# Two weight sums of each MLP half moved from VectorE to adding DMAs on GpSimd's queue, and a new order of the down products

## The chip, the cores and the metric

The kernel runs on one core of one Trainium2 chip. The metric is the device time of one execution in microseconds (us); lower is better. The engines are TensorE (PE, its weight loads PEld), VectorE (DVE), ScalarE (ACT), GpSimd (POOL) and SyncE (SP), each with an instruction stream that it works off in order, and 16 DMA engines that move data between the chip's memory and the on-chip buffers.

## The reference, cut to what matters

A trunk of two decoder layers over 512 tokens of width 1024: layer 0 mixes with multi-head latent attention, layer 1 with gated linear attention; behind each mixer stands an MLP with 4096 hidden units.

```
def sq_relu_mlp(xn, w_up, w_down):
    hid = jnp.square(jax.nn.relu(xn @ w_up))
    return hid @ w_down
...
x = x + mix
x = x + sq_relu_mlp(rms_norm(x, norm_mlp[i]), mlp_w_up[i], mlp_w_down[i])
```

The change touches the two MLPs alone (and the helper that prepares their inputs).

## The kernel before, in words

Every float32 operand of a large matmul is split into a high and a low part (`split`, L112 and L115): ACT copies the operand to the rounded type (`wh`), and DVE subtracts that copy from the operand (`wl`). Three matmuls (high by high, high by low, low by high) then stand for one. `piece` does this for one weight tile; it has three buffers for `wh` and `wl`.

The MLP takes its 4096 hidden units in 8 blocks of 512 (numbered b = 0 to 7), and multiplies in the seven-product scheme of Strassen and Winograd, which needs sums of quarters of the weight matrix. A weight block is cut into quarters: "11" (upper rows, first columns), "12" (lower rows, first columns), "21" (upper rows, second columns) and "22" (lower rows, second columns); in the code `a11`, `a12`, `a21`, `a22` for the up weights.

**Up, per block.** `up_block` gives a list of steps, s1, s5, s2, s6, s3, s7, s4, each with one product of 24 matmuls (L818, 128x128 weights by 256 columns). Its weights are, in turn: a11; `s` = a21 + a22 (summed by DVE, L904, in s5); a12; `s` - a11 (L919, s6); a12 - `s` (L925, s3); a11 - a21 (L932, s7); a22 (s4). Each quarter is 512 KB and is loaded by SP (L852) into one of five buffers (`raw`); a load waits until its buffer's last reader is done. For blocks 0 and 1 the quarters a21 and a22 come together, in one 1 MB load (L1116) into a buffer of the down weights, which are free at that time. Behind the products DVE forms the hidden values (L862, L928, L935: rectified and scaled by the token's `rstd`) and ACT squares them (L863). s4's product goes on in the PSUM bank that s7's product left, so it can begin only when DVE has read that bank in L935.

**Down, per two blocks.** `down_block` has seven products of 48 matmuls, p1, p5, p6, p7, p2, p3, p4, on quarters of 1 MB (SP, L950, three buffers). DVE sums weights for four of them: L987 ("21" + "22" into `S`), L992 (`S` - "11"), L1004 ("11" - "21"), L1019 ("12" - `S`), and hidden values for four (L988, L993, L1005, L1024). There are three such blocks per MLP; the last two hidden blocks go through plain matmuls.

The steps of up and down are interleaved by a fixed list: while down block s is multiplied, up blocks 2s+2 and 2s+3 are. The order on each engine is that in which the code issues; `issue_after` and `keep_in_program_order` pin single places. The layers' inputs for the seven products (`T0` to `T3`, four chunks of sums of token halves) are made in `combine` (L294 to L301) during the output projection before the MLP.

Of the kernel before, what the change touches and what calls it, by code (L numbers as in the profile page):

```python
# [49 lines left out]
def trunk_kernel(ctx: ExitStack, tc: tile.TileContext, t_in: dict, out: bass.AP, out_row: bass.AP):  # L50
# [40 lines left out]
    PADS = dict(stage=224, right=64, up=320, masks=256, keep=128, hidden=(0, 0), down_w=(224, 224))  # L91

    def pad(pool, n):
        if n:
# [3 lines left out]
        pad(opened("stage"), PADS["stage"])  # L98

    opened_stage()  # L100
    pad(opened("edge", "right"), PADS["right"])
    opened("wide", "right")
    opened("ps", space=bass.MemoryType.PSUM)

# [102 lines left out]
    def gcol(name, j):  # L207
        c = GAIN_COL[name] + j
        return gains[:, c : c + 1]
# [56 lines left out]
    class QuadNorm(Norm):  # L266
# [24 lines left out]

        def combine(self, k, t):
            g1, g2 = (gcol(self.g, self.g0 + j) for j in (k, k + KH))
            u, v = xT[k], xT[k + KH]  # L294
# [3 lines left out]
            DVE.scalar_tensor_tensor(t2, u[:, first], g1, t3, ALU.mult, ALU.add)  # L298
            DVE.scalar_tensor_tensor(t4, v[:, first], g2, t2, ALU.mult, ALU.subtract)
            DVE.scalar_tensor_tensor(t1, v[:, second], g2, t2, ALU.mult, ALU.subtract)  # L300
            return t  # L301

        def difference(self, k):
            DVE.tensor_tensor(xT[k][:, second], xT[k][:, second], xT[k + KH][:, second], ALU.subtract)

        def combined(self, k, t):
            pool = pool_of("up")
# [478 lines left out]
    def out_proj(w2d, X, nxt, after, begun=None):  # L786
        for c in range(4):
            if c == 0:
                ps_, rest = begun or out_start(w2d, X, 0)
                rest()  # L790
            else:
                w = out_cols(w2d, c)
                if c == 3:
                    next(after)
                ps_ = [bank("ac"[c % 2]), bank("ac"[c % 2])]
                for j in range(2):
                    a_type(ps_[j], w[j], X)
            for j in range(2):
                m = c + j * KH
                DVE.tensor_tensor(xT[m], ps_[j], xT[m], ALU.add)  # L800
                nxt.add(m, xT[m])
            if c < 3:
                nxt.pair(c)
                nxt.difference(c)


    def mlp(layer, nrm, nxt, final=False):
# [2 lines left out]
        NB = FF // FB  # L810
        up = pool_of("up")

        def wide_raw():
            return pool_of("down_w").tile([P, 4, 512], F32, tag="raw", bufs=3, name=uname("raw"))

        def matmuls(p, w, k0, ks, ms, x, begin, end):
            def one(i, j, k, m, start, stop):
# [15 lines left out]
            for k, m in steps:  # L833
                one(1, 0, k, m, False, end and k == 3)

        Q, wide, turn = {}, {}, [0, 1]

        def up_block(b):
            fh, s = b % 2, b // 2
# [6 lines left out]
            def unit(half, trail):  # L846
                if half and b < 2:
                    return wide[b][:, trail * KH : trail * KH + KH]
                t = up.tile([P, KH, 256], F32, tag="raw", bufs=5, name=uname("raw"))
                c0 = b * FB + half * 256  # L850
                with tc.issue_after(wide["last"].ins) if wide else nullcontext():
                    SP.dma_start(t, w_up[trail * 512 : trail * 512 + 512, c0 : c0 + 256].rearrange("(k p) n -> p k n", p=P))  # L852
                return t

            def product(p, a, name, begin):
                w = v.pop(name) if name in v else piece(a, KH, 256)
# [2 lines left out]
            def finish(c, half, tk):  # L859
                qs = q[tk is second][:, 2 * half : 2 * half + 2]  # L860
                r = nrm.rstd[:, tk].unsqueeze(1).to_broadcast([P, 2, TH])
                DVE.scalar_tensor_tensor(qs, c, 0.0, r, ALU.max, ALU.mult)  # L862
                ACT.activation(qs, qs, AF.Square)  # L863

            def pairs(t):
# [33 lines left out]

            def s5():  # L900
                s = v["s"] = up.tile([P, KH, 256], F32, tag="raw", bufs=5, name=uname("raw"))
                if "a12" not in v:
                    v["a12"] = unit(0, 1)
                DVE.tensor_tensor(s, v["a21"], v["a22"], ALU.add)  # L904
# [11 lines left out]
            def s6():  # L916
                if b == 1:
                    seed(v["p1"])
                DVE.tensor_tensor(v["s"], v["s"], v["a11"], ALU.subtract)  # L919
                product(v["b2"], v["s"], "T2", False)  # L920
                v["u2"] = mt()
                ACT.activation(v["u2"], v["b2"], AF.Copy)

            def s3():
                DVE.tensor_tensor(v["a12"], v["a12"], v["s"], ALU.subtract)  # L925
                product(v["x5"], v["a12"], "22", False)
                c = q[1][:, 0:2]
                DVE.tensor_tensor(c, pairs(v["x5"]), pairs(v["u2"]), ALU.add)  # L928
                finish(c, 0, second)

            def s7():
                DVE.tensor_tensor(v["a21"], v["a11"], v["a21"], ALU.subtract)  # L932
                product(v["b2"], v["a21"], "T3", False)
                c = q[1][:, 2:4]
                DVE.tensor_tensor(c, pairs(v["b2"]), pairs(v["p5"]), ALU.add)  # L935
                finish(c, 1, second)
# [7 lines left out]
        def down_block(s):  # L944
            last = s == NB // 2 - 2

            def quarter(dh, fh):
                t = wide_raw()
                r0 = (2 * s + fh) * FB
                SP.dma_start(t, w_dn[r0 : r0 + FB, dh * 512 : dh * 512 + 512].rearrange("(k p) n -> p k n", p=P))  # L950
                return t

            def operand(t):
# [7 lines left out]
            def product(n, a, t, evac=None):  # L961
                x = operand(t)
                p = mp.tile([P, 4 * TH], F32, tag="d", bufs=2, name=uname("ps"))
                p4 = p.rearrange("p (m t) -> p m t", m=4)
                begin = s == 0
                if not begin:
                    ACT.activation(p4, acc[n], AF.Copy)
                for h in range(2):
                    w = piece(a[:, 2 * h : 2 * h + 2], 2, 512)
                    matmuls(p, w, 2 * h, (2 * h, 2 * h + 1), range(4), x, begin, True)  # L970
                if evac is not None:
                    evac(p4)
                elif begin and n in (2, 3, 4, 5):
                    DVE.tensor_tensor(acc[n], p4, acc[n], ALU.add)
                else:
                    ACT.activation(acc[n], p4, AF.Copy)

# [1 line left out]
            (b11, b12), (b21, b22) = Q[s, 0], Q[s, 1]  # L979

            def p1():
                v["11"] = quarter(0, 0)
                product(1, v["11"], b11)

            def p5():
                v["21"], v["S"] = quarter(1, 0), quarter(1, 1)
                DVE.tensor_tensor(v["S"], v["21"], v["S"], ALU.add)  # L987
                DVE.tensor_tensor(b11, b12, b11, ALU.subtract)  # L988
                product(5, v["S"], b11)

            def p6():
                DVE.tensor_tensor(v["S"], v["S"], v["11"], ALU.subtract)  # L992
                DVE.tensor_tensor(b11, b22, b11, ALU.subtract)  # L993

                def u2(p4):
                    DVE.tensor_tensor(acc[6], p4, acc[1], ALU.add)
# [4 lines left out]
                product(6, v["S"], b11, u2 if last else None)  # L1001

            def p7():
                DVE.tensor_tensor(v["21"], v["11"], v["21"], ALU.subtract)  # L1004
                DVE.tensor_tensor(b12, b22, b12, ALU.subtract)  # L1005

                def u3(p4):
# [3 lines left out]

                product(7, v["21"], b12, u3 if last else None)

            def p2():
                v["12"] = quarter(0, 1)
                product(2, v["12"], b21)

            def p3():
                DVE.tensor_tensor(v["S"], v["12"], v["S"], ALU.subtract)  # L1019
                product(3, v["S"], b22)  # L1020

            def p4():
                a = quarter(1, 1)
                DVE.tensor_tensor(b21, b21, b11, ALU.subtract)  # L1024
                product(4, a, b21)

            return [p1, p5, p6, p7, p2, p3, p4]

        def hidden(b, pool):
            n = 1 if final else 2  # L1030
# [11 lines left out]
        def down(b, hid):  # L1042
            for c in range(2):
                raw = raw_rows(b, c)
                for g in range(2):
# [3 lines left out]
                    for j in range(2):  # L1049
                        m = c * 4 + g * 2 + j  # L1050
                        p = bank("b")
                        a_type(p, w, hid, cols=slice(j * P, (j + 1) * P))
                        DVE.tensor_tensor(xT[m], p, xT[m], ALU.add)
                        if b == NB - 1:
                            nxt.add(m, xT[m])

# [54 lines left out]
            x = quad["11"][0][0]  # L1111
            PE.matmul(t[:, h * TH : (h + 1) * TH], x[:, :P], x, start=h == 0, stop=True, skip_group_check=True)
        for b in range(2):
            t = wide[b] = wide_raw().rearrange("p a (b n) -> p (a b) n", b=2)
            c0 = b * FB + 256
            wide["last"] = SP.dma_start(t, w_up[:, c0 : c0 + 256].rearrange("(k p) n -> p k n", p=P))  # L1116
        kept = tc.keep_in_program_order
        for b in range(2):
            blocks[b].pop(0)()
# [4 lines left out]
        kept(nrm.combined(KH - 1, t))  # L1124
        pad(up, PADS["up"])
        nrm.finish()
        nrm.difference(KH - 1)
        for b in range(2):
            blocks[b].pop(0)()
        downs = []  # L1130
# [419 lines left out]
    turns = rope_turns()  # L1550

    O, begun = mla(0, nrm, w0, mla_pools)
    rope_es.close()
# [160 lines left out]
```

## Time and profile before

| what | value |
|---|---|
| time, median of 3 runs | 1083.45 us (1081.42 to 1085.34) |
| the profiled execution's own time | 1080.79 us |
| its span, first to last instruction | 1079.1 us |
| mean granted TensorE clock | 0.997 |
| PE busy | 1058.9 us (98%), 7322 matmuls |
| DVE busy | 890.0 us (82%) |
| ACT busy | 640.2 us (59%) |
| POOL busy | 44.5 us (4%) |
| moved by DMA | 107.88 MB, mean 100 GB/s |

The span is the time on the engines; the device time is 1.7 us longer. The page gives for each engine its busy time and share, then groups of equal instructions; "idle before" is how long an engine stood still just before an instruction, and behind the arrow stands what it waited for. Layer 0's MLP lies at about 193 to 450 us of the span, layer 1's at about 746 to 1006 us.

### The profile page before, as it was taken

The numbers are of one execution on the slowest core, as the hardware profiler recorded it, in microseconds if no ns is written. First come the engines' busy times: TensorE is split into PE (matmuls) and PEld (weight loads), VectorE is DVE, ScalarE is ACT, GpSimd is POOL, SyncE is SP. The second block draws the span as 40 slices with busy tenths as digits, with TensorE's granted clock in tenths as the row PEclk, the third lists the DMA queues.
The fourth block names the chain that finished last, engine by engine and source line by source line (L and its number), as shares of the span: only waits on it lengthen the run. The fifth ranks groups of instructions, "written<-read, shape, count | busy, mean of one in ns | idle before, by whom it ended". The sixth has DMA issues, their size and how long they took to land.

```text
span 1079.1 us, 17824 instructions
## 1 busy us (share of the span) xinstructions
PE 1058.9 (98%) x7322; PEld 977.1 (91%) x7322; DVE 890.0 (82%) x1210; ACT 640.2 (59%) x934; POOL 44.5 (4%) x78
## 2 busy tenths in 40 slices
PE   9999999989999999999999999999899999999997
PEld 7788888989999999988788888888899999999986
DVE  6789879999899899967565655678999899899865
ACT  6577655566667776644334735655565667766734
POOL 6400000000000000030000000000000000000000
PEclk9999999999999999999999999999999999999999
DMA  7312017143433433260222222234324423522412
GB/s 211 95 49 79 13 31 229 42 136 99 157 98 99 157 100 96 86 203 24 62 67 78 79 79 57 61 98 138 117 79 129 146 82 134 176 76 82 137 39 79
DMA packets 97969, 107.88 MB, mean 100 GB/s; under 512 B 8048, under 2 KB 72832, under 8 KB 97888
## 3 DMA queue, kind: packets, MB, share of 16 engines
q1 hardware_dynamic: 95872, 105.52, 31.1%
q8 instruction: 57, 0.93, 0.4%
q10 hardware_dynamic: 1952, 1.21, 0.4%
q0 software_dynamic: 64, 0.02, 0.1%
q14 instruction: 24, 0.20, 0.1%
HBM read 104.64 MB, written 2.10 MB: 99 GB/s over the span
## 4 chain that ended last, share of the span: by engine, by line
PE 84%; DVE 11%; issue 2%; ACT 2%; DMA 1%; SPq 0%; DVEq 0%; ACTq 0%
PE ps L818 39%; PE ps L120 12%; PE ps L122 12%; PE ps L121 12%; DVE wl L115 4%; PE ps L137 2%; PE ps L1371 2%; DMA wraw_ckv<-in_mla_w_in_dram 1%; DVE q L862 1%; DVE h L115 1%; DVE raw L925 1%; ACT wh L112 1%; DVE raw L932 1%; DVE raw L904 0%; PE ps L1408 0%
## 5 line engine op out<-in xcount | busy, mean ns | idle before, releaser
L112 ACT ACTIVATE wh<-raw 128x1024 fp32r<-128x1024 f32 x208 | 218.9, 1057 | 155.2 <-PE ps L818 84.3
L115 DVE TENSOR_TENSOR wl<-raw,wh 128x1024 fp32r<-128x1024 f32 x208 | 251.8, 1218 | 16.6 <-ACT wh L112 16.3
L818 PE MATMUL ps<-h,wh 128*128 128x256 f32 x1344 | 170.6, 279 | 0.0
L818 PEld LDWEIGHTS ps<-h,wh 128*128 128x128 f32 x1344 | 163.0, 188 | 0.0
L818 PE MATMUL ps<-h,wl 128*128 128x256 f32 x672 | 92.3, 279 | 2.1 <-DVE wl L115 2.1
L120 PE MATMUL ps<-set,wh 128*128 128x512 f32 x232 | 92.0, 397 | 0.7 <-ACT set L245 0.7
L121 PE MATMUL ps<-set,wh 128*128 128x512 f32 x232 | 91.2, 393 | 0.6 <-DVE set L246 0.6
L122 PE MATMUL ps<-set,wl 128*128 128x512 f32 x232 | 91.1, 393 | 0.0
L112 ACT ACTIVATE wh<-wraw 128x1024 fp32r<-128x1024 f32 x41 | 43.0, 1056 | 74.0 <-PE ps L122 41.5
L818 PEld LDWEIGHTS ps<-h,wl 128*128 128x128 f32 x672 | 84.5, 188 | 2.5 <-DVE wl L115 2.5
L863 ACT ACTIVATE q<-q 128x512 f32<-128x512 f32 x64 | 40.0, 629 | 46.4 <-DVE q L862 46.2
L120 PE MATMUL ps<-wh,set 128*128 128x512 f32 x144 | 59.7, 414 | 0.0
L115 DVE TENSOR_TENSOR wl<-wraw,wh 128x1024 fp32r<-128x1024 f32 x41 | 50.3, 1230 | 10.7 <-ACT wh L112 10.6
L115 DVE TENSOR_TENSOR h<-q,h 128x1024 fp32r<-128x1024 f32 x44 | 53.6, 1220 | 4.9 <-ACT h L112 4.9
L122 PE MATMUL ps<-wh,set 128*128 128x512 f32 x144 | 56.3, 391 | 0.0
L121 PE MATMUL ps<-wl,set 128*128 128x512 f32 x144 | 56.3, 391 | 0.0
L121 PEld LDWEIGHTS ps<-set,wh 128*128 128x128 f32 x232 | 44.0, 190 | 10.5 <-DVE set L246 1.3
L120 PEld LDWEIGHTS ps<-set,wh 128*128 128x128 f32 x232 | 43.9, 190 | 10.0 <-ACT set L245 1.0
L122 PEld LDWEIGHTS ps<-set,wl 128*128 128x128 f32 x232 | 44.0, 190 | 9.0
L112 ACT ACTIVATE h<-q 128x1024 fp32r<-128x1024 f32 x44 | 46.2, 1052 | 4.8 <-DVE q L988 2.1
L818 PE MATMUL ps<-T0h,wh 128*128 128x256 f32 x128 | 33.2, 283 | 7.1 <-DVE q L935 6.7
L120 PE MATMUL ps<-hh,wh 128*128 128x512 f32 x96 | 37.4, 389 | 0.0
(512 smaller groups left out, 2778.2 us busy)
## 6 DMA issues: line engine op xcount, KB each, us to landing
raw<-in_mlp_w_down_dram SPq DMA_DIRECT2D x38, 1024.0 KB, 5.2
raw<-in_mlp_w_up_dram SPq DMA_DIRECT2D x56, 512.0 KB, 3.9
wraw<-in_gla_w_in_dram SPq DMA_DIRECT2D x11, 1024.0 KB, 5.1
wraw<-in_mla_w_o_dram SPq DMA_DIRECT2D x8, 512.0 KB, 4.8
raw<-in_mlp_w_up_dram SPq DMA_DIRECT2D x4, 1024.0 KB, 8.0
wraw<-in_gla_w_o_dram SPq DMA_DIRECT2D x8, 512.0 KB, 4.9
xT<-in_x_dram SPq DMA_DIRECT2D x6, 256.0 KB, 7.5
wraw_qn<-in_mla_w_uq_dram SPq DMA_DIRECT2D x6, 256.0 KB, 3.4
```

The lines of the kernel that those rows point to most:

```text
L112: raised.append(order(ACT.activation(hi, src, AF.Copy)))
L115: return lo_eng.tensor_tensor(lo, src, f(hi), ALU.subtract)
L120: PE.matmul(psum, wh, xh, start=start, stop=False, **kw)
L121: PE.matmul(psum, wh, xl, start=False, stop=False, **kw)
L122: PE.matmul(psum, wl, xh, start=False, stop=stop, **kw)
L137: PE.transpose(psum, src, ident[: src.shape[0], : src.shape[0]])
L818: return PE.matmul(p[:, m * TH : (m + 1) * TH], w[i][:, k - k0, m * P : (m + 1) * P], x[k][j], start=start, stop=stop, skip_group_check=True,)
L862: DVE.scalar_tensor_tensor(qs, c, 0.0, r, ALU.max, ALU.mult)
L863: ACT.activation(qs, qs, AF.Square)
L925: DVE.tensor_tensor(v["a12"], v["a12"], v["s"], ALU.subtract)
L932: DVE.tensor_tensor(v["a21"], v["a11"], v["a21"], ALU.subtract)
L1371: PE.matmul(p[:, t * 64 : (t + 1) * 64].rearrange("p (n c) -> p n c", c=m), k[:, sl], later, start=True, stop=True)
```

## The change

Two sums per up block and two per down block are no longer made by DVE. Instead SP loads the first summand into the tile, and a DMA on GpSimd's queue adds the second summand to it on the way from memory (`accum_op=ALU.add`). In an up block these are `s` = a21 + a22 (a new tile fill: SP reloads a21, POOL adds a22) and a21 + a11 (POOL adds a11 to the a21 tile, in place of L932's difference). In a down block they are `S` = "22" + "21" and "21" + "11"; "22" is loaded again for p4. These DMAs can only add, so differences become sums: the inputs' lower rows are negated (a tile of negated gains, `gains_less`; sums in place of differences; the lower half is rectified by a minimum in place of a maximum; two accumulators are subtracted). The down products go in the order 1, 5, 6, 7, 4, 2, 3. In the first two blocks the 1 MB loads become two of 512 KB. The core of it:

```diff
-                DVE.tensor_tensor(s, v["a21"], v["a22"], ALU.add)
+                with tc.issue_after(wide["last"].ins):
+                    SP.dma_start(s, rows(1, 0))
+                POOL.dma_start(s, rows(1, 1), accum_op=ALU.add)
...
+            def fill(t, half, trail):
+                with tc.issue_after(wide["last"].ins) if "last" in wide and b > 1 else nullcontext():
+                    i = SP.dma_start(t, rows(half, trail))
+                if half and not trail:
+                    POOL.dma_start(t, rows(0, 0), accum_op=ALU.add)
...
             def s7():
-                DVE.tensor_tensor(v["a21"], v["a11"], v["a21"], ALU.subtract)
                 product(v["b2"], v["a21"], "T3", False)
...
             def p1():
-                v["11"] = quarter(0, 0)
+                v["S"] = quarter(x, 1, 1, (1, 0))
+                v["11"] = quarter(y, 0, 0)
+                v["21"] = quarter(z, 1, 0, (0, 0))
                 product(1, v["11"], b11)
 
             def p5():
-                v["21"], v["S"] = quarter(1, 0), quarter(1, 1)
-                DVE.tensor_tensor(v["S"], v["21"], v["S"], ALU.add)
-                DVE.tensor_tensor(b11, b12, b11, ALU.subtract)
+                DVE.tensor_tensor(b11, b11, b12, ALU.subtract)
...
             def p7():
-                DVE.tensor_tensor(v["21"], v["11"], v["21"], ALU.subtract)
+                v["22"] = quarter(y, 1, 1)
...
-            return [p1, p5, p6, p7, p2, p3, p4]
+            return [p1, p5, p6, p7, p4, p2, p3]
```

The changed lines sit some 17 lines lower in the changed code: L862 becomes L879, L919 becomes L938, L925 becomes L944, L935 becomes L953; the new loads and adds of `s` are L920 (SP) and L921 (POOL), the adds to a21 L865, those of the down sums L975.

Over the whole program PE's matmuls stay as they are, in the same order. DVE has 44 sums fewer (32 of 128x1024, 12 of 128x2048), and one small instruction more. POOL has 44 DMAs more (32 of 512 KB, 12 of 1 MB), SP 16 loads more net.

Three places on which the prediction rests. The first is ACT at the start of layer 0's MLP. Here raw_2390 is block 0's `s` before, raw_2395 after; q_... are hidden values; wh_... are high parts. Before:

```order
L131 ACTIVATE mt_2330<-mt_2328 128x512
L112 ACTIVATE wh_2393<-raw_2390 128x1024
L112 ACTIVATE wh_2424<-raw_2390 128x1024
L863 ACTIVATE q_2252<-q_2252 128x512
L863 ACTIVATE q_2281<-q_2281 128x512
```

And after:

```order
L131 ACTIVATE mt_2335<-mt_2333 128x512
L880 ACTIVATE q_2257<-q_2257 128x512
L880 ACTIVATE q_2286<-q_2286 128x512
L112 ACTIVATE wh_2399<-raw_2395 128x1024
L112 ACTIVATE wh_2430<-raw_2395 128x1024
```

The high part of block 0's `s`, which PE's product s5 reads, stood ahead of the two squares, and stands behind them now.

The second place is DVE a little later, where block 1's `s` (raw_2548 before, raw_2553 after) comes in. Before:

```order
L928 TENSOR_TENSOR q_2253<-ps_2392,mt_2452 128x512
L115 TENSOR_TENSOR wl_2519<-raw_2248,wh_2518 128x1024
L862 SCALAR_TENSOR_TENSOR q_2253<-q_2253,rstd_2327 128x512
L115 TENSOR_TENSOR wl_2552<-raw_2548,wh_2551 128x1024
L935 TENSOR_TENSOR q_2253<-ps_2279,mt_2421 128x512
L919 TENSOR_TENSOR raw_2548<-raw_2548,raw_2156 128x1024
```

And after:

```order
L115 TENSOR_TENSOR wl_2524<-raw_2249,wh_2523 128x1024
L947 TENSOR_TENSOR q_2258<-ps_2398,mt_2458 128x512
L115 TENSOR_TENSOR wl_2558<-raw_2553,wh_2557 128x1024
L879 SCALAR_TENSOR_TENSOR q_2258<-q_2258,rstd_2332 128x512
L938 TENSOR_TENSOR raw_2553<-raw_2553,raw_2157 128x1024
L953 TENSOR_TENSOR q_2258<-ps_2284,mt_2427 128x512
```

In both, s4 of block 0 waits for the reading of the PSUM bank (L935, now L953), and the split of block 1's `s` (`wl`) stands ahead of that reading. Before, the split stood directly ahead and its operand was DVE's own earlier sum; now an L879 and an L938 have come between, and the operand is made by DMAs of SP and POOL.

The third is those two queues at the start of the MLP. SP after (raw_2249 and raw_2253 hold a21 and a22 of blocks 0 and 1, raw_2395 and raw_2553 their `s`):

```order
L863 DMA raw_2249<-in_mlp_w_up_dram 128x4x256 x2
L863 DMA raw_2253<-in_mlp_w_up_dram 128x4x256 x2
L920 DMA raw_2395<-in_mlp_w_up_dram 128x4x256
L973 DMA raw_2792<-in_mlp_w_down_dram 128x4x512
L920 DMA raw_2553<-in_mlp_w_up_dram 128x4x256
```

And POOL after, which had no DMA there before:

```order
L865 DMA raw_2249<-in_mlp_w_up_dram 128x4x256
L865 DMA raw_2253<-in_mlp_w_up_dram 128x4x256
L921 DMA raw_2395<-in_mlp_w_up_dram 128x4x256
L921 DMA raw_2553<-in_mlp_w_up_dram 128x4x256
L865 DMA raw_2717<-in_mlp_w_up_dram 128x4x256
```

Each of POOL's adds waits for SP's load into the same tile. There are five buffers for the up quarters; block 1's `s` is the sixth tile of that kind, and takes the buffer of block 0's a11, whose last reader is block 0's L938.

More of the change, by code (lines that the diff above doesn't have):

```diff
@@ L100, in trunk_kernel @@
     opened_stage()
-    pad(opened("edge", "right"), PADS["right"])
+    less = opened("edge", "right").tile([P, 16], F32, name="gains_less")
     opened("wide", "right")
@@ L293, in combine @@
             g1, g2 = (gcol(self.g, self.g0 + j) for j in (k, k + KH))
+            l1, l2 = (less[:, self.g0 + j : self.g0 + j + 1] for j in (k, k + KH))
             u, v = xT[k], xT[k + KH]
@@ L811, in mlp, with wide_raw @@
         up = pool_of("up")
-        def wide_raw():
-            return pool_of("down_w").tile([P, 4, 512], F32, tag="raw", bufs=3, name=uname("raw"))
+        ring = ["w0", "w2", "w1"]
+        def wide_raw(tag=None):
+            if tag is None:
+                tag = ring.pop(0)
+                ring.append(tag)
+            return pool_of("down_w").tile([P, 4, 512], F32, tag=tag, name=uname("raw"))
         def matmuls(p, w, k0, ks, ms, x, begin, end):
@@ L848, in unit, with rows @@
                     return wide[b][:, trail * KH : trail * KH + KH]
-                t = up.tile([P, KH, 256], F32, tag="raw", bufs=5, name=uname("raw"))
+                return fill(up.tile([P, KH, 256], F32, tag="raw", bufs=5, name=uname("raw")), half, trail)
+            def rows(half, trail):
                 c0 = b * FB + half * 256
-                with tc.issue_after(wide["last"].ins) if wide else nullcontext():
-                    SP.dma_start(t, w_up[trail * 512 : trail * 512 + 512, c0 : c0 + 256].rearrange("(k p) n -> p k n", p=P))
+                return w_up[trail * 512 : trail * 512 + 512, c0 : c0 + 256].rearrange("(k p) n -> p k n", p=P)
+            def fill(t, half, trail):
[3 more added lines that the diff above has]
+                    POOL.dma_start(t, rows(0, 0), accum_op=ALU.add)
+                if half and b < 2:
+                    wide["last"] = i
                 return t
+            fills.append(fill)
             def product(p, a, name, begin):
@@ L861, in finish @@
                 r = nrm.rstd[:, tk].unsqueeze(1).to_broadcast([P, 2, TH])
[L862 removed]
+                DVE.scalar_tensor_tensor(qs, c, 0.0, r, ALU.min if half else ALU.max, ALU.mult)
                 ACT.activation(qs, qs, AF.Square)
@@ L918, in s6 @@
                     seed(v["p1"])
-                DVE.tensor_tensor(v["s"], v["s"], v["a11"], ALU.subtract)
+                DVE.tensor_tensor(v["s"], v["s"], v["a11"], ALU.add)
                 product(v["b2"], v["s"], "T2", False)
@@ L924, in s3 @@
             def s3():
-                DVE.tensor_tensor(v["a12"], v["a12"], v["s"], ALU.subtract)
+                DVE.tensor_tensor(v["a12"], v["a12"], v["s"], ALU.add)
                 product(v["x5"], v["a12"], "22", False)
@@ L945, in down_block, with rows, quarter @@
             last = s == NB // 2 - 2
-            def quarter(dh, fh):
-                t = wide_raw()
+            x, y, z = ring
+            def rows(dh, fh):
                 r0 = (2 * s + fh) * FB
-                SP.dma_start(t, w_dn[r0 : r0 + FB, dh * 512 : dh * 512 + 512].rearrange("(k p) n -> p k n", p=P))
+                return w_dn[r0 : r0 + FB, dh * 512 : dh * 512 + 512].rearrange("(k p) n -> p k n", p=P)
+            def quarter(tag, dh, fh, more=None):
+                t = wide_raw(tag)
+                SP.dma_start(t, rows(dh, fh))
+                if more:
+                    POOL.dma_start(t, rows(*more), accum_op=ALU.add)
                 return t
@@ L973, in product @@
                 elif begin and n in (2, 3, 4, 5):
-                    DVE.tensor_tensor(acc[n], p4, acc[n], ALU.add)
+                    DVE.tensor_tensor(acc[n], p4, acc[n], ALU.add if n < 4 else ALU.subtract)
                 else:
@@ L1052, in down @@
                         a_type(p, w, hid, cols=slice(j * P, (j + 1) * P))
-                        DVE.tensor_tensor(xT[m], p, xT[m], ALU.add)
+                        DVE.tensor_tensor(xT[m], p, xT[m], ALU.subtract if b < NB - 1 and m >= KH else ALU.add)
                         if b == NB - 1:
@@ L1126, in mlp @@
         nrm.finish()
-        nrm.difference(KH - 1)
+        nrm.total(KH - 1)
         for b in range(2):
@@ L1550, in trunk_kernel @@
     turns = rope_turns()
+    DVE.tensor_scalar(less, gains[:, GAIN_COL["mlp"] : GAIN_COL["mlp"] + 16], -1.0, None, ALU.mult)
     O, begun = mla(0, nrm, w0, mla_pools)
```

40 lines of the change are left out of this document (20 added, 20 removed).

## The prediction

> **What bounds the kernel now.** I read the page's busy row and its chain first:
>
> ```profile
> PE 1058.9 (98%) x7322; PEld 977.1 (91%) x7322; DVE 890.0 (82%) x1210; ACT 640.2 (59%) x934; POOL 44.5 (4%) x78
> PE 84%; DVE 11%; issue 2%; ACT 2%; DMA 1%; SPq 0%; DVEq 0%; ACTq 0%
> ```
>
> PE is busy for 98% of the span of 1079.1 us, and the chain of waits runs through PE for 84% and through DVE for 11%. The table of windows says where that is, with the columns length, then PE, PEld, DVE, ACT and POOL busy, granted clock, DMA share and GB/s:
>
> ```profile
> 200.00:250.00 50.00, 46.22 (x395) 45.49 (x394) 49.93 (x50) 29.59 (x37) 0.00 (x0) 1.00 0.34 106
> 250.00:300.00 50.00, 50.00 (x437) 50.00 (x436) 45.47 (x43) 29.72 (x34) 0.00 (x0) 1.00 0.39 127
> 300.00:350.00 50.00, 50.00 (x436) 50.00 (x435) 49.81 (x44) 33.48 (x38) 0.00 (x0) 1.00 0.34 106
> ```
>
> Once layer 0's MLP has started, PE has no gap: 437 matmuls in 50 us, 114.4 ns each, so 2.75 us for a product of 24. DVE is nearly full too, but it is not late. Only the start (200 to 250 us) has gaps, and there DVE is busy for 49.93 of 50 us. What PE's MLP matmuls wait for in the whole program (total, times, longest) is this:
>
> ```profile
> PE ps L818 <- DVE q L935: 6.7, 4, 2.0
> PE ps L818 <- DVE wl L115: 2.4, 3, 1.1
> PE ps L818 <- ACT wh L112: 1.4, 3, 0.5
> ```
>
> That is 10.5 us, 1.0% of the span, and the ceiling of what a lighter DVE can return. The four waits for L935 are the starts of the two MLPs (s4 of blocks 0 and 1 of each); the three for `wl` are two at the ends and one small one in layer 1.
>
> **What the change takes away.** The sums, by the rows of DVE's groups:
>
> ```profile
> L932 DVE TENSOR_TENSOR raw<-raw,raw 128x1024 f32<-128x1024 f32 x16 | 19.5, 1219 | 0.1
> L987 DVE TENSOR_TENSOR raw<-raw,raw 128x2048 f32<-128x2048 f32 x6 | 13.7, 2286 | 1.3 <-DMA raw<-in_mlp_w_down_dram 1.2
> L1004 DVE TENSOR_TENSOR raw<-raw,raw 128x2048 f32<-128x2048 f32 x6 | 13.7, 2283 | 0.0
> ```
>
> With L904's 16 of the same size as L932's, DVE loses 32 x 1.219 + 12 x 2.285 = 66.4 us, 33 per MLP. In the saturated middle that is worth nothing: PE is late for no one. The sums and negations that stay or change their sign cost DVE what they did before; the down order 1, 5, 6, 7, 4, 2, 3 leaves PE's work as it is. At the ends of the MLPs a DVE that has 33 us less behind it should no longer be waited for: I credit the whole `wl` row, **-2.4 us**.
>
> **What it adds in the middle.** Block b+1's `s` was one DVE instruction on two tiles long there. Now a chain makes it: SP's load, POOL's add (X us from issue to landing), ACT's `wh`.
>
> ```profile
> L112 ACT ACTIVATE wh<-raw 128x1024 fp32r<-128x1024 f32 x208 | 218.9, 1057 | 155.2 <-PE ps L818 84.3
> raw<-in_mlp_w_up_dram SPq DMA_DIRECT2D x56, 512.0 KB, 3.9
> raw<-in_mlp_w_down_dram SPq DMA_DIRECT2D x38, 1024.0 KB, 5.2
> pos_i<-in_positions_dram POOLq DMA_DIRECT2D x1, 2.0 KB, 4.5
> invf<-in_inv_freq_dram POOLq DMA_DIRECT2D x1, 16.0 KB, 6.9
> ```
>
> Its buffer is free when the split of block b's a21 tile (for s7) is done. From there to s5 of block b+1, PE's own work from an even to an odd block is s7, p6, s4, s1: 2.75 + 5.5 + 2.75 + 2.75 = 13.75 us, from odd to even one down product more. The split leads PE by up to 3 us when DVE is early, so the budget is 14 to 17 us; the chain costs 3.9 + X + 1.06. It is hidden while X stays under about 9 to 12; I take 10.5. Three such tight places per MLP, six in all, each cost X - 10.5 beyond that. The adds to a21 and the two down sums have a block or more of slack.
>
> X is the unknown: no trace row shows an adding DMA. The bounds are POOL's two rows, 4.5 and 6.9 us for tiny transfers (during the loads at the program's beginning). For size, SP's rows say that 512 KB more cost 5.2 - 3.9 = 1.3 us, and an adding DMA reads twice, which speaks for the upper half; the load of that beginning speaks for the lower. I take the middle, **X = 5.7**. The Trainium skill ("DMA: Bandwidth & Descriptors", section "Anatomy of one DMA") has a fit for GpSimd's DMAs, 2.0 us plus the bytes over 436 KB per us, which would be 3.2 us for 512 KB; no row here shows a DMA of that queue under 4.5, and by this fit the sum below would be 0 in place of +5.
>
> The added traffic is 16 reloads and 32 adds of 512 KB and 12 adds of 1 MB, some 37 MB on 107.9. In the MLP's windows the DMA share is 0.27 to 0.43, so the engines have room; contention shows in X alone.
>
> **What it does at the start of each MLP.** These rows of the timeline (start, length, instruction) are the start of layer 0's:
>
> ```profile
> 202.84 0.40 PE L818 MATMUL ps<-x7h,wl 128*128 128x256 f32 x2
> 203.08 0.28 PE L818 MATMUL ps<-T0h,wh 128*128 128x256 f32 x1
> ...
> 199.46 1.06 ACT L112 ACTIVATE wh<-raw 128x1024 fp32r<-128x1024 f32 x1 [0.48 <-DVE raw L904]
> 205.69 1.14 ACT L863 ACTIVATE q<-q 128x512 f32<-128x512 f32 x2
> ...
> 203.41 1.22 DVE L919 TENSOR_TENSOR raw<-raw,raw 128x1024 f32<-128x1024 f32 x1
> 204.55 1.28 DVE L862 SCALAR_TENSOR_TENSOR q<-ps,rstd 128x512 f32<-128x512 f32 x2
> 208.10 1.22 DVE L904 TENSOR_TENSOR raw<-raw 128x1024 f32<-128x1024 f32 x1
> 216.19 0.68 DVE L935 TENSOR_TENSOR q<-ps,mt 128x512 f32<-128x512 f32 x1
> ...
> 217.02 0.36 PE L818 MATMUL ps<-T0h,wh 128*128 128x256 f32 x1 [1.77 <-DVE q L935]
> ```
>
> The last product on a12 (x7h) ends at 203.24, and s5 of block 0 (T0h) follows at once, since its `wh` was made at 199.46. After the change that `wh` stands behind two squares, and the second square waits for L879 of the product that ends at 203.24. So: L879 0.65, square 0.6, `wh` 1.06, which is 205.6: s5 of block 0 starts 2.5 us later. Then the chain for block 1's `s`: `wl` 1.2 (206.8), L938 1.2 (208.0), which frees the buffer, SP's load 3.9 (211.9), POOL's add X, `wh` 1.06, `wl` 1.15, L879 0.6, L938 1.15, L953 0.6, all in DVE's order ahead of s4 of block 0. That is 211.9 + X + 4.6 plus some 0.2 of hand-overs = **216.7 + X**, 222.4 with X = 5.7, where it was 217.02: +5.4. PE's products in between (s5, s6, s3, s7: 4 x 2.8) end at 217 and hide none of the rest. From s4 of block 0 to s4 of block 1 there are five products and one L935:
>
> ```profile
> 230.74 0.39 PE L818 MATMUL ps<-T3h,wl 128*128 128x256 f32 x2
> 232.66 0.39 PE L818 MATMUL ps<-T0h,wh 128*128 128x256 f32 x1 [1.53 <-DVE q L935]
> ```
>
> They take 231.13 - 217.02 = 14.1 plus 0.6 for L953 at once, 14.7, in place of 15.64: 0.9 comes back. Layer 0's start: **+4.5**.
>
> Layer 1's start repeats it:
>
> ```profile
> 755.58 0.40 PE L818 MATMUL ps<-x7h,wl 128*128 128x256 f32 x2
> 770.39 0.36 PE L818 MATMUL ps<-T0h,wh 128*128 128x256 f32 x1 [1.97 <-DVE q L935]
> 787.26 0.39 PE L818 MATMUL ps<-T0h,wh 128*128 128x256 f32 x1 [1.40 <-DVE q L935]
> 770.00:775.00 5.00, 4.61 (x26) 4.64 (x27) 4.25 (x5) 2.64 (x3) 0.00 (x0) 0.66 0.87 297
> ```
>
> From the last a12 product's end the same steps give 755.98 + (216.7 - 203.24) + X = 769.4 + X = 775.1, which is +4.7 on 770.39. The 16.87 us to 787.26 hold a stretch of lower granted clock (0.66 over 5 us: 1.7 us lost); without it they are 15.2, and 14.7 follow after the change. That is **+4.2** if the stretch comes again, +2.5 if not; I take the middle, +3.4.
>
> **The sum.** +4.5 + 3.4 - 2.4 = +5.5, of which I take **+5**, for some of the waits for `wh` (1.4) falls into the new, longer wait. On the profiled execution that is 1080.8 + 5 = 1085.8. That execution was 2.7 us faster than the median of the runs, 1083.45, and below them all; carried to the median the time is **1088.5 us**. X stands in both starts, so as a formula the change is 2X - 6.4: +2.6 with X = 4.5, +7.4 with 6.9. A measurement of this kernel tells 0.3% (3.3 us) from no change.
>
> **The rivals.**
> *The adds land as fast as plain loads* (X = 3.9 or less). Then the starts cost what they did: +1.4, and with X = 3.2, 0. For it: SP's row of 3.9; against it: POOL's rows. With the lower-clock stretch gone as well it is -1. This is "no change".
>
> *DVE's relief wins.* If the two squares do not hold s5 of block 0 back, because DVE and ACT come through the start earlier than I worked out, the 2.5 us go out of both starts: s4 of block 0 is then due at 214.2 + X, and the change is 2X - 11.4. From X = 4 down that is a gain over 0.3%; with X = 3.2 it is -5, or **1078**. For it: DVE is at 49.93 of 50 us exactly where PE waits, and four sums of 1.22 us of the first 20 us go. Against it: the second square needs the product that ends at 203.24, whatever DVE does, and POOL's rows begin at 4.5.
>
> *The adds are slow in the middle* (X over 10.5, by two reads and a write through one queue, or since POOL must make descriptors while DVE is busy). Then the six tight places stall. X = 12 gives 2 x 12 - 6.4 + 6 x 1.5 = +27, 1110; X = 9, without a stall there, +12, 1095. For it: GpSimd's 16 KB took 6.9; against: the page's DMA share leaves room. The Trainium skill ("SBUF — State Buffer") says that GpSimd cannot write DMA descriptors while DVE holds their shared port in certain copy and scalar modes; the sums and splits here are two-tensor operations, and no run here shows such a wait.
>
> *The adds do not take DVE's place, but the same data wait for buffers:* five `raw` buffers now hold `s` from its load on, not from its sum on, so loads of the next block could come late. SP's loads are 10 us and more ahead of their readers in the middle; I see no case that costs over 1 us, and give it nothing of its own.
>
> **How the numbers follow.** Slower by the start chain (X from 4.8 to 9): 0.42. Slow adds, X over 9: 0.10, which also ends slower. No change (X up to 4.8, or the terms fall a little lower): 0.28. Faster by over 0.3%: 0.20. So slower is 0.52, same 0.28, faster 0.20. The range reaches from the relief's 1078 to X = 10.5 in both starts (+14.6, so 1098, and 1099 for what is rounded); beyond it lie about 0.07 on the slow side and 0.08 on the fast one. The likeliest case's own range is 1086.7 to 1091 (X from 4.8 to 6.9).
>
> **What would show it.** In the changed kernel's timeline, s5 of block 0 starts about 2.5 us behind the last a12 product, with a wait for ACT's `wh`; s4 of block 0 waits some 4 us for L953, and DVE's idle time ahead of block 1's `wl` falls in SP's load plus POOL's add. The DMA rows give X for 512 KB directly. From 250 us on PE has 437 matmuls in 50 us as before; if a window there has fewer, with waits behind s5 of odd blocks, the adds are slow. If s4 of block 0 comes at 218 or earlier, the start chain was wrong and the kernel is not slower.

## The result, and the profile after

The changed kernel takes 1113.38 us (median of 4 runs, 1112.24 to 1117.6) against 1083.63 us before on the same chip: a ratio of 1.0283, 95% interval 1.025 to 1.0316. It is slower by 30 us, where the forecast was +5 and the range ended at +15.5. The profiled execution took 1114.01 us, its span is 1112.3, 33.2 us more than before.

The page's busy row, the rows of the DMA queues and the chain answer to those of before:

```profile
PE 1065.8 (96%) x7322; PEld 981.9 (88%) x7322; DVE 833.1 (75%) x1167; ACT 637.6 (57%) x934; POOL 101.0 (9%) x122
q0 software_dynamic: 23296, 29.38, 16.8%
PE 71%; DVE 12%; DMA 11%; ACT 2%; issue 2%; SPq 0%; DVEq 0%; ACTq 0%; POOLq 0%
PE ps L824 28%; PE ps L120 12%; PE ps L122 12%; PE ps L121 12%; DMA raw<-in_mlp_w_up_dram 11%; DVE wl L115 5%; ACT wh L112 2%; PE ps L1396 2%; PE ps L137 1%; DVE h L115 1%; DMA wraw_ckv<-in_mla_w_in_dram 1%; DVE raw L938 1%; DVE raw L1017 1%; DVE q L879 1%; PE ps L1433 0%
```

DVE is indeed lighter by 57 us. But a link that the chain of before did not have now holds 11% of the span: the DMAs of the up weights. GpSimd's queue holds 16.8% of the engines' time. What PE's MLP matmuls wait for (total, times, longest), and the DMA rows (count, size, us from issue to landing):

```profile
PE ps L824 <- DVE q L953: 17.1, 4, 7.9
PE ps L824 <- ACT wh L112: 11.4, 9, 2.4
PE ps L824 <- ACT ps L992: 5.9, 2, 3.1
PE ps L824 <- DVE wl L115: 1.6, 5, 0.5
...
raw<-in_mlp_w_up_dram SPq DMA_DIRECT2D x80, 512.0 KB, 5.6
raw<-in_mlp_w_down_dram SPq DMA_DIRECT2D x38, 1024.0 KB, 6.3
raw<-in_mlp_w_up_dram POOLq DMA_DIRECT2D x32, 512.0 KB, 7.1
raw<-in_mlp_w_down_dram POOLq DMA_DIRECT2D x12, 1024.0 KB, 10.5
```

So X is 7.1 us in the median, and SP's plain loads went from 3.9 to 5.6 us. The start of layer 0's MLP, on PE, DVE and ACT (start, length, instruction, idle time before it and what ended it):

```profile
206.39 0.39 PE L824 MATMUL ps<-T0h,wh 128*128 128x256 f32 x1 [2.39 <-ACT wh L112]
226.30 0.58 PE L824 MATMUL ps<-T0h,wh 128*128 128x256 f32 x1 [7.49 <-DVE q L953]
242.62 0.39 PE L824 MATMUL ps<-T0h,wh 128*128 128x256 f32 x1 [0.86 <-DVE q L953]
...
222.68 1.23 DVE L115 TENSOR_TENSOR wl<-raw,wh 128x1024 fp32r<-128x1024 f32 x1 [5.90 <-ACT wh L112]
225.56 0.68 DVE L953 TENSOR_TENSOR q<-ps,mt 128x512 f32<-128x512 f32 x1
...
221.59 1.06 ACT L112 ACTIVATE wh<-raw 128x1024 fp32r<-128x1024 f32 x1 [7.45 <-DMA raw<-in_mlp_w_up_dram]
...
213.13 1.27 POOL L921 DMA_DIRECT2D raw<-in_mlp_w_up_dram  x1 [16.30 <-DMA raw<-in_mlp_w_up_dram]
```

ACT stands still for 7.45 us behind the DMA, DVE for 5.90 behind ACT, PE for 7.49 behind DVE: one chain seen from three engines. Both kernels run the same 7322 matmuls in the same order, so the start of each can be set against its start before. The distance is 0.8 us ahead of the MLP of layer 0; it grows by 9.2 us at the start of that MLP, by 2.5 in its middle and by 3.5 at its end; by 8.2, 7.2 and 2.2 us in layer 1. That is 17.4 us at the starts, 9.7 in the middles and 5.7 at the ends.

### The profile page after: what moved, and what is told of

Its sections match the earlier page's. It is cut to its first block, busy times and chain, and to the rows that moved or that the text cites. A ratio compares the mean times of both kernels' runs of the same rounds, so it can differ in the third digit from the quotient of the medians.

```text
span 1112.3 us, 17956 instructions
## 1 busy us (share of the span) xinstructions
PE 1065.8 (96%) x7322; PEld 981.9 (88%) x7322; DVE 833.1 (75%) x1167; ACT 637.6 (57%) x934; POOL 101.0 (9%) x122
## 3 DMA queue, kind: packets, MB, share of 16 engines
q0 software_dynamic: 23296, 29.38, 16.8%
## 4 chain that ended last, share of the span: by engine, by line
PE 71%; DVE 12%; DMA 11%; ACT 2%; issue 2%; SPq 0%; DVEq 0%; ACTq 0%; POOLq 0%
PE ps L824 28%; PE ps L120 12%; PE ps L122 12%; PE ps L121 12%; DMA raw<-in_mlp_w_up_dram 11%; DVE wl L115 5%; ACT wh L112 2%; PE ps L1396 2%; PE ps L137 1%; DVE h L115 1%; DMA wraw_ckv<-in_mla_w_in_dram 1%; DVE raw L938 1%; DVE raw L1017 1%; DVE q L879 1%; PE ps L1433 0%
## 5 line engine op out<-in xcount | busy, mean ns | idle before, releaser
L865 POOL DMA_DIRECT2D raw<-in_mlp_w_up_dram x16 | 20.7, 1292 | 519.6 <-DMA raw<-in_mlp_w_up_dram 258.5
L824 PE MATMUL ps<-T0h,wh 128*128 128x256 f32 x128 | 34.7, 294 | 27.4 <-DVE q L953 17.1
L115 DVE TENSOR_TENSOR wl<-wraw,wh 128x1024 fp32r<-128x1024 f32 x41 | 50.3, 1229 | 10.6 <-ACT wh L112 10.4
L824 PEld LDWEIGHTS ps<-T0h,wh 128*128 128x128 f32 x128 | 24.7, 193 | 29.7 <-DVE q L953 17.9
## 6 DMA issues: line engine op xcount, KB each, us to landing
raw<-in_mlp_w_down_dram POOLq DMA_DIRECT2D x12, 1024.0 KB, 10.5
```

The source lines that it names most:

```text
L115: return lo_eng.tensor_tensor(lo, src, f(hi), ALU.subtract)
L824: return PE.matmul(p[:, m * TH : (m + 1) * TH], w[i][:, k - k0, m * P : (m + 1) * P], x[k][j], start=start, stop=stop, skip_group_check=True,)
L865: POOL.dma_start(t, rows(0, 0), accum_op=ALU.add)
```

## The experiments

Times are medians; each ratio is to the kernel before on the same chip, with its 95% interval.

**1. Only the down sums by adding DMA.**

```diff
-                POOL.dma_start(s, rows(1, 1), accum_op=ALU.add)
+                DVE.tensor_tensor(s, v["a21"], v["a22"], ALU.add)
...
             def s7():
+                DVE.tensor_tensor(v["a21"], v["a21"], v["a11"], ALU.add)
```

(SP's reload of `s` and the adds to a21 go as well.) Expected:

> The changed kernel with the up sums (21+22 and 11+21) back on DVE; the adding DMAs of the down sums and the order 1, 5, 6, 7, 4, 2, 3 stay. My theory: of the 32.8 us that the trace of the changed kernel lost, 17.4 (starts) and 9.7 (middles) hang on the chain load, add, split of s, and go; 5.7 at the ends belong to the new down order and stay, so about 1089 us, with no PE wait at s5. Rival, traffic: the loss goes with the bytes added (12 MB of 37 stay), so about 1093 us, with slower PE products everywhere in the middle.

Measured: 1080.39 us, 0.9979 (0.9968 to 0.999). The up adds carry all of the loss, and more than my theory said: the ends' 5.7 us, which I had put down to the new down order, are gone too, though that order is still there. The wait for L992 (ACT's copy of an accumulator into the PSUM bank, behind which product 4 begins; L997 here) is 0.6 us in all; in the changed kernel it is 5.9.

**2. Only the up sums by adding DMA.** The down products are as before: DVE sums, old order, no DMA of GpSimd.

```diff
-                v["S"] = quarter(x, 1, 1, (1, 0))
-                v["11"] = quarter(y, 0, 0)
-                v["21"] = quarter(z, 1, 0, (0, 0))
+                v["11"] = quarter(0, 0)
...
+                v["21"], v["S"] = quarter(1, 0), quarter(1, 1)
+                DVE.tensor_tensor(v["S"], v["21"], v["S"], ALU.add)
```

> The changed kernel with the down products as before (sums on DVE, order 1, 5, 6, 7, 2, 3, 4); the up sums stay on adding DMAs. My theory: the ends' 5.7 us go and little else, about 1107 us, and the starts' waits for L953 stay at 7 to 8 us. Rival, contention: the 1 MB adds are what stretches the loads and adds of s (7.4 us in the median); then X falls to about 5 and the loss to about 10 us, 1094 us.

Measured: 1112.0 us, 1.0269 (1.0221 to 1.0318). X stays at 7.1 us without one 1 MB add on the queue; the waits for L953 are 16.6 us in all. The rival falls. My theory's second half stays open: the trace has no wait for L992 any more, and its ends are 2.6 us shorter than before the change, not 5.7 longer; but the total hardly moves, and its interval (1106 to 1116 us) holds the 1107 of my theory as well as no effect.

**3. The old down order, all adds kept.**

```diff
-                v["22"] = quarter(y, 1, 1)
+                v["12"] = quarter(y, 0, 1)
...
-            return [p1, p5, p6, p7, p4, p2, p3]
+            return [p1, p5, p6, p7, p2, p3, p4]
```

> The changed kernel with the down products in the order 1, 5, 6, 7, 2, 3, 4, all adding DMAs kept. My theory: product 4, put right behind 7, must wait until DVE has added product 7 into its accumulator (PE waits for ACT's copy of it, 2.9 and 3.1 us, and a stretch of lower clock behind one); with two products between, both waits go: about 5.7 us less, 1107.7 us. Rival: the ends are late because the adds are, whatever the order: 1113 us, and the wait for L992 is found at another product.

Measured: 1119.55 us, 1.0341 (1.031 to 1.0372). The waits for L992 are gone as I expected, but the kernel is 6 us slower, not faster (the two intervals just touch): the waits for `wh` rose from 11.4 to 20.7 us. One of four like places, at blocks 4 and 6 of each layer, where the add of `s` follows a 1 MB add on GpSimd's queue:

```profile
311.21 1.28 POOL L975 DMA_DIRECT2D raw<-in_mlp_w_down_dram  x1 [9.11 <-DMA raw<-in_mlp_w_down_dram]
314.06 1.28 POOL L921 DMA_DIRECT2D raw<-in_mlp_w_up_dram  x1 [1.57 <-DVE wl L115]
...
329.82 2.01 ACT L112 ACTIVATE wh<-raw 128x1024 fp32r<-128x1024 f32 x2 [7.65 <-DMA raw<-in_mlp_w_up_dram]
```

A 1 MB add is issued at 311.21, the add of `s` 2.9 us behind it, and ACT gets `s` at 329.8: 15.7 us for 512 KB. In the changed kernel the same two stand 6 us apart (304.9 and 310.8) and the second takes 9.3. The new order is not a fault in itself: it keeps the 1 MB adds out of the way of `s`. My reading of the ends as a cost of the order is refuted as a statement on time.

**4. The sums of blocks 0 and 1 on DVE.** As experiment 1, but for `b < 2` only.

> The changed kernel with the up sums of blocks 0 and 1 alone back on DVE (plain loads there). My theory: the chain for block 1's s is all of the loss at the starts, 17.4 us, so about 1096 us, and the waits for L953 fall to under 2 us each. Rival, order: ACT and DVE now hold s back behind the squares and L938, whoever makes the sum; then 2.5 us per start and more stay, about 1102 us.

Measured: 1105.46 us, 1.0217 (1.0188 to 1.0246). The four waits for L953 (L958 here) fall from 17.1 to 7.0 us, as before the change (6.7). But only 7 of the 17 us come back. In the trace the starts lose 6.4 us in place of 17.4 (the `s` of block 2 is late now: PE waits 0.4 us for it in layer 0, 2.0 in layer 1), but the middles lose 12.2 in place of 9.7, and the ends 7.2 in place of 5.7. Taking the chain out of one place moves a part of the wait to the next.

**5. The same DMAs, without the adding.**

```diff
-                    POOL.dma_start(t, rows(0, 0), accum_op=ALU.add)
+                    POOL.dma_start(t, rows(0, 0))
```

(and so for the other two.)

> The changed kernel with its 44 DMAs on GpSimd's queue as plain loads: they overwrite the tile in place of adding, so the sums are left out; order, waits, sizes and queue stay. If the adding itself (a second read of the tile) makes X long, X falls from 7.1 to about 4.5 to 5 us for 512 KB, and with two starts and some ten tight places the time falls by 8 to 15 us, to about 1100. If it is the queue (descriptors made by GpSimd, the shared engines), X stays within 0.7 us and the time within 4 us of 1113.

Measured: 1093.48 us, 1.0107 (1.0086 to 1.0128): 19 of the 30 us are the adding. The rows of the DMAs, and of the queue:

```profile
raw<-in_mlp_w_up_dram SPq DMA_DIRECT2D x80, 512.0 KB, 4.6
raw<-in_mlp_w_up_dram POOLq DMA_DIRECT2D x32, 512.0 KB, 4.6
raw<-in_mlp_w_down_dram POOLq DMA_DIRECT2D x12, 1024.0 KB, 6.1
...
q0 software_dynamic: 7936, 29.38, 8.5%
```

For the same 29.38 MB the queue takes 8.5% of the engines' time in place of 16.8%, and 7936 packets in place of 23296; X is 4.6 in place of 7.1 us, for 1 MB 6.1 in place of 10.5; and SP's loads beside it are faster (4.6, not 5.6). The middle has no wait left. Set against the kernel before, matmul by matmul, this kernel loses 13.3 us at the starts and none in the middles or at the ends: the adding is worth 4 us of the starts' 17.4, and all of the rest. At the starts the serial chain remains:

```profile
PE ps L824 <- DVE q L953: 11.0, 4, 4.9
PE ps L824 <- ACT wh L112: 4.8, 2, 2.4
```

**6. Both at once**, experiments 4 and 5 together.

> The changed kernel with the up sums of blocks 0 and 1 on DVE, and all other DMAs of GpSimd's queue as plain loads (those sums are left out). If the adding's extra time and the chain at the starts are all of the loss, nothing is left: 1080 to 1085 us. If the added traffic or the serial load behind load still cost in the middle, 1088 us or more.

Measured: 1080.19 us, 0.9985 (0.9974 to 0.9997). Nothing of the loss is left, with the same loads behind loads for `s` of blocks 2 to 7. So the added bytes and the serial load cost nothing in the middle, as long as X is about 4.5.

**7. `s` alone by adding DMA**, a21 + a11 back on DVE.

```diff
-                if half and not trail:
-                    POOL.dma_start(t, rows(0, 0), accum_op=ALU.add)
...
             def s7():
+                DVE.tensor_tensor(v["a21"], v["a21"], v["a11"], ALU.add)
```

> The changed kernel with a21 + a11 back on DVE; only s = a21 + a22 (and the down sums) come by adding DMAs. My theory now: the chain load, add, split of s carries the whole loss, so 1108 to 1114 us, with the waits for L953 still 7 to 8 us each. Rival: the 16 adds to a21, ahead of s in GpSimd's line and beside it on the engines, carry a good part; then about 1098 us and X of s near 6 us.

Measured: 1109.51 us, 1.0237 (1.0213 to 1.0261). Half as many up adds, and nearly the whole loss: the chain for `s` carries it. The adds to a21 are worth some 5 us at most; the intervals of the two kernels touch.

**8 and 9. a21 + a11 by adding DMA, no DMA for `s`.** DVE makes both weights from the sum that has come in:

```diff
+                s = v["a11"]
+                DVE.tensor_tensor(t, v["a21"], v["a22"], ALU.add)
+                DVE.tensor_tensor(s, t, s, ALU.subtract)
...
-                DVE.tensor_tensor(v["s"], v["s"], v["a11"], ALU.add)
```

With the down products of before:

> Up: a21 + a11 by adding DMA as in the changed kernel, but no DMA for s: DVE makes s + a11 as (a21 + a11) + a22, which s6 needs anyway, and takes a11 off again for s5, so three DVE sums per block where the kernel before has four. Down: as before (DVE, old order). My theory: no wait of PE hangs on an add any more, so the time is at most that of before, 1079 to 1083 us. Rival, contention: 8 MB per MLP of adds alone slow the plain loads enough to be waited for; 1086 us or more.

With those of the changed kernel:

> The same with the down products of the changed kernel (adding DMAs, order 1, 5, 6, 7, 4, 2, 3). The kernel with only these down adds was at 0.9979 of before. My theory: both reliefs of DVE add up where it was waited for (ends: 2.4 us; starts: a part of 6.7), so 1077 to 1080 us. Rival, contention of the 512 KB and the 1 MB adds: slower than either alone, 1083 us or more.

Measured: 1085.9 us, 1.0024 (1.001 to 1.0038), and 1084.49 us, 1.0015 (1.0003 to 1.0027). Both miss. No add is made into `s`, yet s5 now needs two sums in a row ahead of its split, and PE waits 0.5 to 0.9 us at s5 and again at its low-part matmuls, at the starts and, in the first of the two kernels, for the last block. And the wait for an add is not gone: the first of the two sums (L922) reads the a21 tile that a DMA adds to. In the second kernel this add landed 8.8 us after its issue in layer 0, DVE stood for it, and s4 of block 1 waited 4.8 us where it waited 1.5 before:

```profile
225.34 1.23 DVE L922 TENSOR_TENSOR raw<-raw,raw 128x1024 f32<-128x1024 f32 x1 [2.69 <-DMA raw<-in_mlp_w_up_dram]
...
236.46 0.58 PE L824 MATMUL ps<-T0h,wh 128*128 128x256 f32 x1 [4.78 <-DVE q L952]
```

This one place costs 5.3 us in the trace, with a stretch of lower clock behind it, more than any other of that kernel.

**10 and 11. The small gain of experiment 1: adds, order, or the rest?** First everything on DVE in the old order, but with the change's signs, its 512 KB loads at the start and its fixed buffers; then that with the down adds (and the earlier loads of the down quarters that go with them):

```diff
+                if more:
+                    POOL.dma_start(t, rows(*more), accum_op=ALU.add)
```

> All four weight sums back on DVE and the old down order; what stays of the change are the negated rows, the 512 KB loads at the start and the fixed buffers. Within 0.3% of before (1079 to 1085 us) by every theory; it is the base for the next two. If it is at 0.998 of before, the small gain of the kernel with adding DMAs for the down sums alone came from these, and not from the adds or the order.

> Up sums on DVE, down sums by adding DMAs, old order 1, 5, 6, 7, 2, 3, 4. If the gain (0.9979 with the new order) comes from DVE's relief, it stays: 1079 to 1081 us. If the new order is what hides the adds, the old one waits for a 1 MB add (10 us) at products 5 or 7: 1084 us or more.

Measured: 1080.51 us, 0.9989 (0.998 to 0.9998), and **1078.03 us, 0.9966 (0.9955 to 0.9978)**, the fastest kernel of this study. The down adds, with their loads, are worth some 2.5 us, in the old order. Its page:

```profile
PE 1057.0 (98%) x7322; PEld 975.3 (91%) x7322; DVE 867.2 (81%) x1199; ACT 640.6 (60%) x934; POOL 58.6 (5%) x90
PE ps L824 <- DVE q L958: 6.6, 4, 1.8
raw<-in_mlp_w_down_dram POOLq DMA_DIRECT2D x12, 1024.0 KB, 9.5
```

The wait for `wl` at the ends (2.1 us in the kernel of experiment 10) is gone from its list. A 1 MB add takes 9.5 us here, and no one waits for it.

**12. The sum a21 + a11 of blocks 0 and 1 on GpSimd as an instruction**, on top of experiment 1.

```diff
-                DVE.tensor_tensor(v["a21"], v["a21"], v["a11"], ALU.add)
+                (POOL if b < 2 else DVE).tensor_tensor(v["a21"], v["a21"], v["a11"], ALU.add)
```

> The kernel with adding DMAs for the down sums and the new order, and a21 + a11 of blocks 0 and 1 as a sum on GpSimd in place of DVE. My theory: the starts' waits for the reading of the PSUM bank (6.7 us) are DVE's queue of work, so two sums of 1.1 us less there give 1 to 3 us, 1077 to 1079 us. Rival: GpSimd's sum (a quarter of the size took 0.81 us) is slow, or holds DVE up at the memory's port, and nothing is won or 1 to 3 us lost.

Measured: 1090.51 us, 1.0083 (1.0067 to 1.0099), 10 us more than experiment 1. While GpSimd adds, DVE stands. DVE and GpSimd:

```profile
199.59 0.69 DVE L218 SCALAR_TENSOR_TENSOR mt<-ps,mt 128x512 f32<-128x512 f32 x1
200.31 2.62 DVE L220 SCALAR_TENSOR_TENSOR mt<-mt,mt 128x512 f32<-128x512 f32 x1
202.85 1.21 DVE L115 TENSOR_TENSOR wl<-raw,wh 128x1024 fp32r<-128x1024 f32 x1
...
199.99 2.39 POOL L954 TENSOR_TENSOR raw<-raw,raw 128x1024 f32<-128x1024 f32 x1 [117.50 <-PE ps L824]
```

L220 takes 0.68 us in experiment 1, and 2.62 here: it ends 0.55 us after GpSimd's 2.39 us are over. The Trainium skill ("SBUF — State Buffer", section "Who interferes with whom") says that a DVE instruction with two inputs in this memory contends with a GpSimd instruction that reads it, and calls the port that they share an exclusive lock. L220 reads two such tiles; the trace agrees, since it takes about its usual time from the end of GpSimd's sum on.

## Why the prediction was wrong

The direction was right, the size was not: +5 forecast, +30 measured, outside the range.

**The step that failed is the price of an adding DMA, X = 5.7, with bounds of 4.5 and 6.9.** It was the middle of two tiny plain DMAs of GpSimd's queue; neither the 1.3 us for size nor the second read was added to it. Experiment 5 shows what was left out: a plain 512 KB DMA on that queue takes 4.6 us, just above the lower bound, and the adding puts 2.5 us on it, and 4.4 on 1 MB. I had written that an adding DMA reads twice, and then let the load of the program's beginning weigh against it. The Trainium skill's fit ("DMA: Bandwidth & Descriptors", section "Anatomy of one DMA") gave an estimate of 3.2 us, below even the plain DMA; here the measurement decides.

The trace lost 32.8 us where the terms of the sum said 5.5: 9.5 more at the starts, 9.7 in the middles and 8.1 at the ends. Put into the formula 2X - 6.4, the measured 7.1 would give only +8; the rest of the miss lies in what follows.

**The second half of the same step: "contention shows in X alone".** Doubling the queue's engine time also slows the loads beside it. The changed kernel's loads for `s` (the 16 of L920) take 3.7 to 14.1 us, 7.1 in the median, where I put 3.9 (5.4 with the plain DMAs of experiment 5). L920's landings, then those of L921, the adds to `s`:

```profile
DMA to landing us min/median/max: 3.7/7.1/14.1
DMA to landing us min/median/max: 6.0/7.4/9.3
```

Nor did the engines have the room that I saw. I read a DMA share of 0.27 to 0.43 in the windows of 50 us; in the changed kernel it is 0.59 to 0.89, and while block 1's `s` is added it is 1.04 in place of 0.78. The share stands second to last (the first line and the last are the changed kernel's, the one between is of before):

```profile
300.00:350.00 50.00, 50.00 (x436) 50.00 (x435) 44.87 (x42) 32.78 (x36) 5.29 (x5) 1.00 0.89 223
215.00:220.00 5.00, 3.23 (x29) 3.06 (x28) 5.00 (x7) 2.35 (x4) 0.00 (x0) 1.00 0.78 232
215.00:220.00 5.00, 3.81 (x33) 3.60 (x31) 0.79 (x2) 0.00 (x0) 1.27 (x1) 1.00 1.04 201
```

The tight chain in the middle thus costs 7.1 + 7.4 (X for `s`) + 0.6 of hand-overs = 15 us plus `wh`, against a budget that I put at 3.9 + 10.5 = 14.4 plus `wh`. The budget was about right: PE waits around blocks 3, 5 and 7, whose chains take about that. That is the 9.7 us of the middles that I priced at nothing, and experiments 5 and 6 show them gone when X is 4.6 and 4.4. I placed the stalls at odd blocks; the 1.6 us at 976 in layer 1 is an even one, whose load took 14.1 us.

**The start chain held step by step.** s5 of block 0 came 2.4 us behind the last a12 product (I said 2.5). For s4 of block 0 I wrote 216.7 + X. SP's load landed at 212.6, as worked out, the add was issued at 213.13 and landed at 221.5, so X with its hand-over is 8.9; with the 0.8 us by which all of this execution was later, that gives 226.4, and it started at 226.30. In experiment 5 the same X is 6.7, the offset 0.35: 223.75, and the trace has 223.71. So of the 9.5 us that the starts cost over my 7.9, 6.5 are X at its two places (8.9 and 9.0 in place of 5.7). The rest is mostly the granted clock: behind the long wait PE ran at a lower one in both layers, and I had put no price on that in layer 0 and half of one in layer 1. The windows of the changed kernel:

```profile
226.00:231.00 5.00, 4.70 (x27) 4.71 (x28) 3.19 (x5) 2.39 (x3) 0.00 (x0) 0.63 1.02 178
794.00:799.00 5.00, 4.77 (x22) 4.77 (x23) 3.05 (x4) 2.27 (x3) 0.00 (x0) 0.50 0.93 169
```

**The ends: -2.4 credited, +5.7 measured.** The credit itself was right: with the down adds alone (experiment 11) the ends give back 1.4 and 1.3 us. What I missed is that DVE, however light in total, is late when one add is late. In layer 0, DVE waits for block 7's `s` and then has hardly a gap for 17 us, up to the update that product 4's start waits for:

```profile
440.49 1.22 DVE L115 TENSOR_TENSOR wl<-raw,wh 128x1024 fp32r<-128x1024 f32 x1 [4.05 <-ACT wh L112]
455.97 1.22 DVE L1035 TENSOR_TENSOR xT<-xT,sum 128x1024 f32<-128x1024 f32 x1
...
457.22 1.03 ACT L992 ACTIVATE ps<-xT 128x1024 f32<-128x1024 f32 x1 [4.46 <-DVE xT L1035]
458.30 3.70 PE L824 MATMUL ps<-h,wh 128*128 128x256 f32 x16 [2.87 <-ACT ps L992]
```

It takes both the late add and the new order, which puts product 4 directly behind product 7: without the up adds (experiment 1) the wait is 0.6 us; with the old order (experiment 3) it is none, and other waits grow.

**The rivals.** The slow adds, given 0.10, were the case, at a lower X than I asked of them: I took X as one number for all, and priced 1110 us only from X = 12 up, with the loads beside them at 3.9. The fast adds are excluded (X was at least 6.0), and so is DVE's relief as a winner. The last rival, waits for buffers, was given nothing. No kernel here tried a sixth buffer; how much of the chain is the late buffer stays open. What is shown is that adding costs 19 of the 30 us, and that with plain DMAs and the first two blocks' sums on DVE none is left.

## What to carry to other kernels

Price a DMA that adds as its own kind: here it took twice the engine time of a plain one, and slowed its neighbours. Put such sums where the tile has time to spare (the down quarters here, where a 1 MB add took 9.5 us and no one waited), never where a load, an add and a split follow each other on the way to the next product. An engine's busy total says little on when it is late: one late operand in its in-order stream delays all that is behind it.

## What the runs showed of the hardware that was not expected

- Adding makes a DMA much dearer: 512 KB took 4.6 us plain and 7.1 adding, 1 MB 6.1 and 10.5, the queue's engine time doubled (8.5% and 16.8%), its packets went from 7936 to 23296 for equal bytes, and issuing one kept GpSimd for 1.28 us in place of 0.75.
- An add on GpSimd's queue that follows another closely takes much longer: 15.7 us for 512 KB behind a 1 MB add issued 2.9 us earlier, which itself took 13.2 (medians of 6.9 and 10.4 in that kernel). Whether it waits in the queue or shares the engines is not shown.
- A long wait of PE is often followed by 3 to 6 us of half the granted clock (after 7.5, 7.9 and 2.9 us here, costing some 1.7, 2.7 and 1.7 us), but not always: none followed 3.1 us at 1033 in layer 1, and in the kernel before one followed 1.97 us and none 1.77.
